# Conditioning weights of a two-layer decoder step: six vectors, loaded and placed otherwise

## The chip, the cores and the metric

One core of one Trainium2 chip. The metric is the device time of one execution in microseconds. The kernel before took 1056.21 us, the median of three runs (1053.03 to 1056.43).

## The reference

One step of a two-layer trunk for 256 prompt tokens and 8 sample tokens (264 columns, D = 1024). What the change touches is the conditioning at the head of each layer: six vectors of 1024 values for each of nine conditions (one prompt, eight samples), from a weight matrix of 1024 x 6144 (25.2 MB a layer).

```
def _layer(x, c, q_pos, lp, slopes, past):
    mod = einsum('bd,de->be', silu(c), lp['ada_w']) + lp['ada_b']
    sh1, sc1, g1, sh2, sc2, g2 = split(mod, 6)
    h = _rmsnorm(x, lp['norm1_g']) * (1 + sc1) + sh1
    proj = h @ lp['w_in']             # q, compressed/selected/window K and V, gates, z, x/B/C, dt
    kcmp, vcmp = _compress(k/v cache pages + new rows)     # blocks of 32, stride 16, small MLP
    o_att = gated sum of compressed, selected (top 16 blocks) and window attention
    y     = Mamba-2 scan over x/B/C, gated RMSNorm
    x = x + g1 * (concat[o_att, y] @ lp['w_out'])
    h2 = _rmsnorm(x, lp['norm2_g']) * (1 + sc2) + sh2
    ug, uv = split(h2 @ lp['ffn_w_up'])
    x = x + g2 * ((silu(causal_dwconv(ug)) * uv) @ lp['ffn_w_down'])
```

So vectors 0 and 1 (sh1, sc1) are needed before the projections, 2 (g1) at the output projection, 3 and 4 (sh2, sc2) at the second norm, and 5 (g2) at the down projection.

## The kernel before, in words

Activations lie feature by token: x is 128 partitions x 8 chunks x 264 tokens. Each weight tile (128x1024) is split on the chip into a high part (ACT copy, `whi`) and a low part (VectorE subtraction, `wlo`), and a product is three matmuls per chunk (`gemm8`): 24 matmuls of 264 columns to a projection tile.

The conditioning is `ada(l, r)`, a generator: three pieces r of 2048 columns. For each of 8 chunks k of the contraction four loads of 256 KB come in (`ada`, 128x512), and four matmuls with the 128x32 stationary silu(c) (`cs`) go to the four quarters of the array's columns, all into one PSUM bank, `psfl`. The four are a row here; a step of the generator (one `yield`) is a row. After the eighth row an ACT copy (`adam`), four transposes and one VectorE addition (`mod`) hand the piece over.

The stages stand in this order: compression of the cached pages of layer one (`compress`: units of two samples, 48 matmuls into `pso` each, pages in `cpg` tiles), with its first unit at the very start; the norm; projections (`w_in`, 6 + 10 tiles into `psmm`); attention and Mamba as several generators, stepped in the order of a written string SEQ; output projection; feed-forward (22 up pairs of tiles), in which layer two's compression units and its conditioning are stepped; down projection. The tile framework's scheduler then orders each engine's instructions by priority and dependence within these constraints, so the four matmuls of one row may come apart. Conditioning steps are called at: the start (piece 0 of layer one), the projections of layer one (piece 1, as `side`), its attention (piece 2, letter A of SEQ, as `fill`), its feed-forward (piece 0 of layer two, every other f), the down projection (DOWN = 5 rows of piece 1 of layer two), the head of layer two's projections (GAP = 3 rows and the rest as `side`), its attention (piece 2).

ADA_BUFS gives the buffers of the `ada` tag by pool: 6 in the compression pool, 4 in that of attention, 6 in the feed-forward's. Selected-cache pages (`page`) are fetched by `fetch` into a ring of 8. In the Mamba part the eight samples' B and C vectors are spread over partitions by a product with the identity (`bd`) and a ones matmul, one `bd` for each of eight pieces. Every engine instruction is issued by the helper `emit` and the trace gives its line, L117, to nearly all rows; the tile names tell them apart. Names: psfl conditioning, pso compression, psmm projections and other wide products, psat attention and small products.

Of the kernel before, what the change touches and what calls it, by code (L numbers as in the profile page):

```python
# [17 lines left out]
NL = 2  # L18
D = 1024
TP = 256  # L20
NS = 8
# [13 lines left out]
ADA_BUFS = {"cmp": 6, "att": 4, "ffn": 6}  # L35
# [67 lines left out]
def decode_step(ctx, tc, I, O):  # L103
# [199 lines left out]
    def ada(l, r):  # L303

        if r == 0:
# [4 lines left out]
        acc = fl()  # L310
        for k in range(KC):
            for g in range(4):
                name = pools_names[-1]
                t = sb([512], "ada", ADA_BUFS[name[:3]], F32, pools[-2] if name == "attn1" else pools[-1])
                load(t, I["ada"][l, r * KC + k, :, g, :])
                PE.matmul(acc[32 * g:32 * g + 32, :], cs[:, k, :], t, start=k == 0, stop=k == KC - 1)
                if g == 1 and HALF:
                    yield
            yield
        m = sb([512], "adam", 1)  # L320
        S.activation(m, acc, AF.Copy)
        tr = fl()
        for j in range(4):
            PE.transpose(tr[:, j * 128:(j + 1) * 128], m[:, j * 128:(j + 1) * 128], ident)
        V.tensor_tensor(MOD[l][:, r * 16:(r + 1) * 16, :].rearrange("p (g j) m -> p g j m", g=4),
                        tr.rearrange("p (j g m) -> p g j m", j=4, g=4)[:, :, :, 0:9],
                        MOD[l, "b"][:, r * 16:(r + 1) * 16].rearrange("p (g j) -> p g j", g=4)
                        .unsqueeze(3).to_broadcast([128, 4, 4, 9]), op=OP.add)
# [47 lines left out]
    def compress(l, both, bufs):  # L376
# [15 lines left out]
        def pages(s, kv):  # L392
            t = ph([NPG, 2 if both else 1, 128], "cpg", bufs)
            load_pages(t, I["cmpc"][l], s, 0 if both else kv, 2 if both else 1)
# [45 lines left out]
        for kv, sp in order:  # L440
            if kv not in W:
                weights(kv)
            if not both:
                raws = [pages(s, kv)[:, :, 0, :] for s in (2 * sp, 2 * sp + 1)]
            elif kv == 0:
                pair = [pages(s, 0) for s in (2 * sp, 2 * sp + 1)]
# [15 lines left out]
    def layer(l, A, pa, early, done, side, fill):  # L462
# [10 lines left out]
        for _ in range(GAP[l]):  # L473
            next(side, None)

# [110 lines left out]
        done()  # L586
        pb = begin(f"attn{l}")


        def slot(tag, shape, dt=F32):  # L590
            return sb(shape, tag, dict(whi=WB[0], wlo=WB[1], st=WB[2])[tag], dt)

        order = (0, 2, 4, 6, 1, 3, 5, 7)
        ring = []

        def fetch():
            n = len(ring)
            i, s = n // NS, order[n % NS]  # L600
            if i > 2:
                return
            t = ph([1024], "page", PAGES)
            if i == 2:
                load(t, I["wst"][l, s])
                store(O["wst"][l, s], t)
                v = t.rearrange("p (a c f) -> p a c f", a=2, c=4)
                ring.append((v[:, 0], v[:, 1]))
            else:
                v = t.rearrange("p (c a f) -> p c a f", a=2, c=4)  # L610
                load_pages(v, I["slcc"][l], s, 0, 2, 4 * i, 4)
                ring.append((v[:, :, 0, :], v[:, :, 1, :]))

        def samples():
# [24 lines left out]
            for _ in range(PAGES):  # L639
# [416 lines left out]
        def space_samples():  # L1056
# [26 lines left out]
            ys = small([4, NS], 1, "ys")  # L1083
            for g in range(2):
# [5 lines left out]
                for b in range(2):  # L1090
                    o = mb()
                    bd = small([NS, 64], 1, "bd")
                    V.tensor_tensor(bd[:8], bc[:8, b, 64 * g:64 * g + 64].unsqueeze(1).to_broadcast([8, NS, 64]),
                                    ident[:8, :8].unsqueeze(2).to_broadcast([8, NS, 64]), op=OP.mult)
                    PE.matmul(o, ones[:8, :], bd[:8].rearrange("p s n -> p (s n)"), start=True, stop=True)
# [88 lines left out]
        bg = [compress(l + 1, 0, 4), ada(l + 1, 0)] if l + 1 < NL else []  # L1184
        for f in range(NFF):
            if f % 2 == 0:
                for b in bg:
                    for _ in range(1 + UNITS * (f == 0 and b is bg[0])):
                        next(b, None)
# [22 lines left out]
        rest = ada(l + 1, 1) if l + 1 < NL else iter(())  # L1212
# [27 lines left out]
    units, third = compress(0, 1, 4), ada(0, 0)  # L1240
    for i in range(FIRST):
        next(units)
        if i == 0:
            load(cst, I["consts"])
            load(x, I["xT"])
        for _ in range(-(-8 // FIRST)):
            next(third, None)
    run(third)
    for k in range(KC):
        square(k)  # L1250
# [29 lines left out]
GAP = (0, 3)  # L1280
DOWN = 5
UNITS = 0
PINS = ()
HALF = 0
# [128 lines left out]
```

## Time and profile before

| | |
|---|---|
| median of 3 runs | 1056.21 us (1053.03 to 1056.43) |
| the profiled execution | 1060.55 us |
| its span | 1058.8 us |
| mean granted TensorE clock | 0.949 |
| busy: TensorE, VectorE, ACT, POOL | 979.6, 655.8, 486.3, 170.0 us |

The span is what the trace covers. The chain is the sequence of work that ended last, followed back from the last instruction; a stage is read from it by taking the chain of that stretch only. A matmul of the conditioning is two records, so a row of four shows as x8. In the chain "DMA ada" is time in which TensorE waited for a conditioning load and for nothing else.

### The profile page before, as it was taken

The numbers are of one execution on the slowest core, as the hardware profiler recorded it, in microseconds if no ns is written. First come the engines' busy times: TensorE is split into PE (matmuls) and PEld (weight loads), VectorE is DVE, ScalarE is ACT, GpSimd is POOL, SyncE is SP. The second block draws the span as 40 slices with busy tenths as digits, with TensorE's granted clock in tenths as the row PEclk, the third lists the DMA queues.
The fourth block names the chain that finished last, engine by engine and source line by source line (L and its number), as shares of the span: only waits on it lengthen the run. The fifth ranks groups of instructions, "written<-read, shape, count | busy, mean of one in ns | idle before, by whom it ended". The sixth has DMA issues, their size and how long they took to land.

```text
span 1058.8 us, 20737 instructions
## 1 busy us (share of the span) xinstructions
PE 979.6 (93%) x7480; PEld 795.0 (75%) x7480; DVE 655.8 (62%) x1427; ACT 486.3 (46%) x1036; POOL 170.0 (16%) x337
## 2 busy tenths in 40 slices
PE   3799999997997999999999989999799789999996
PEld 3238898652466899899998949965246689999995
DVE  2347554557657865766764558365865777777553
ACT  3225544332254554655553426453235456666441
POOL 0201001114213000101111103031421311111110
PEclk9899999897899899999999999999789889999998
DMA  8779668436847777765577568753694635555651
GB/s 279 262 240 304 227 211 280 162 128 203 333 158 222 225 219 232 255 195 193 185 233 236 165 223 262 250 180 126 207 339 152 208 100 180 181 180 182 195 171 41
DMA packets 115081, 220.33 MB, mean 208 GB/s; under 512 B 13218, under 2 KB 56098, under 8 KB 114850
## 3 DMA queue, kind: packets, MB, share of 16 engines
q1 hardware_dynamic: 110882, 205.29, 60.5%
q0 software_dynamic: 3520, 13.17, 3.1%
q8 instruction: 59, 0.97, 0.4%
q10 hardware_dynamic: 576, 0.54, 0.2%
q14 instruction: 44, 0.36, 0.1%
HBM read 204.70 MB, written 14.25 MB: 207 GB/s over the span
## 4 chain that ended last, share of the span: by engine, by line
PE 82%; DMA 6%; DVE 6%; ACT 2%; issue 2%; SPq 2%; POOL 0%; DVEq 0%; ACTq 0%; POOLq 0%
PE psmm L117 42%; PE psat L117 23%; PE pso L117 10%; PE psfl L117 8%; DMA ada<-in_ada_dram 3%; SPq L117 1%; DMA st<-in_cw_dram 1%; DVE wlo L117 1%; DMA st<-in_wup_dram 1%; DVE bd L117 1%; DMA cpg<-in_cmpc_dram 1%; DVE rs L117 1%; ACT whi L117 1%; DVE psm L117 0%; DVE st L117 0%
## 5 line engine op out<-in xcount | busy, mean ns | idle before, releaser
L117 DVE TENSOR_TENSOR wlo<-st,whi 128x1024 fp32r<-128x1024 f32 (+1 forms) x204 | 232.7, 1141 | 148.8 <-ACT whi L117 132.9
L117 ACT ACTIVATE whi<-st 128x1024 fp32r<-128x1024 f32 (+1 forms) x204 | 201.8, 991 | 231.0 <-PE psmm L117 163.3
L117 PE MATMUL psmm<-hhi,whi 128*128 128x264 f32 x800 | 233.3, 292 | 4.2 <-ACT hhi L117 2.6
L117 PE MATMUL psmm<-hhi,wlo 128*128 128x264 f32 x800 | 228.4, 286 | 0.8 <-DVE wlo L117 0.8
L117 PE MATMUL psmm<-hlo,whi 128*128 128x264 f32 x800 | 228.6, 286 | 0.0
L117 PEld LDWEIGHTS psmm<-hhi,whi 128*128 128x128 f32 x800 | 151.5, 190 | 22.3 <-issue 7.4
L117 PEld LDWEIGHTS psmm<-hhi,wlo 128*128 128x128 f32 x800 | 151.2, 189 | 3.0 <-DVE wlo L117 1.6
L117 PEld LDWEIGHTS psmm<-hlo,whi 128*128 128x128 f32 x800 | 151.9, 190 | 0.9 <-issue 0.7
L117 PE MATMUL psmm<-act,whi 128*128 128x264 f32 x704 | 128.7, 284 | 0.0
L117 PEld LDWEIGHTS psmm<-act,whi 128*128 128x128 f32 x704 | 108.8, 188 | 4.2 <-issue 3.4
L117 PE MATMUL psfl<-ada,cs 128*32 128x512 f32 x384 | 99.3, 648 | 11.0 <-DMA ada<-in_ada_dram 10.9
L117 PE MATMUL psat<-hhi,whi 128*128 128x264 f32 x352 | 100.8, 286 | 1.4 <-ACT whi L117 1.4
L117 PE MATMUL psat<-hhi,wlo 128*128 128x264 f32 x352 | 100.6, 286 | 1.0 <-DVE wlo L117 1.0
L117 PE MATMUL psat<-hlo,whi 128*128 128x264 f32 x352 | 100.5, 286 | 0.0
L117 PE MATMUL psmm<-act,wlo 128*128 128x264 f32 x352 | 99.9, 284 | 0.0
L117 PE MATMUL pso<-whi,cwh 128*128 128x252 f32 x256 | 76.3, 298 | 21.0 <-ACT whi L117 16.2
L117 PE MATMUL pso<-wlo,cwh 128*128 128x252 f32 x256 | 75.5, 295 | 0.1
L117 PE MATMUL pso<-whi,cwl 128*128 128x252 f32 x256 | 75.3, 294 | 0.0
L117 PEld LDWEIGHTS pso<-whi,cwh 128*128 128x128 f32 x256 | 51.3, 200 | 31.6 <-ACT whi L117 16.2
L117 PEld LDWEIGHTS psat<-hhi,whi 128*128 128x128 f32 x352 | 67.1, 191 | 1.6 <-ACT whi L117 1.6
L117 PEld LDWEIGHTS psat<-hhi,wlo 128*128 128x128 f32 x352 | 66.8, 190 | 1.2 <-DVE wlo L117 1.2
L117 PEld LDWEIGHTS psat<-hlo,whi 128*128 128x128 f32 x352 | 67.2, 191 | 0.0
(303 smaller groups left out, 1553.2 us busy)
## 6 DMA issues: line engine op xcount, KB each, us to landing
ada<-in_ada_dram SPq DMA_DIRECT2D x192, 256.0 KB, 4.4
st<-in_wup_dram SPq DMA_DIRECT2D x88, 512.0 KB, 3.6
st<-in_wdn_dram SPq DMA_DIRECT2D x44, 512.0 KB, 3.5
st<-in_win_dram SPq DMA_DIRECT2D x40, 512.0 KB, 4.6
page<-in_slcc_dram SPq DMA_DIRECT2D x128, 128.0 KB, 2.6
st<-in_cw_dram SPq DMA_DIRECT2D x16, 512.0 KB, 5.4
cpg<-in_cmpc_dram SPq DMA_DIRECT2D x64, 128.0 KB, 3.3
st<-in_wout_dram SPq DMA_DIRECT2D x32, 256.0 KB, 3.0
```

The lines of the kernel that those rows point to most:

```text
L117: ins = f(*a, **k)
```

## The change

Conditioning is computed in six vectors j of 1024 columns. A load is 128 x 4 x 256 floats (512 KB): one chunk k with all four quarters. Two chunks make a pair, which the new helper `together` issues as eight adjacent matmuls, those of the tile loaded later first. With `wide`, a pair lives in one of the page tiles (`cpg`, 4 buffers), else in two `ada` buffers; ADA_BUFS is now 3, 2 and 4. A step of the generator is a pair, four to a vector; each vector has a hand-off with two transposes.

The places: vectors 0 and 1 of layer one at the start, ahead of all pages and weights, x loaded first of all; 2 and 3 in its projections; 4 in its attention; 5 in its feed-forward, followed there by 0 and 1 of layer two; 2 of layer two in the down projection (DOWN = 4); 3 and 4 in layer two's projections; 5 in layer two's feed-forward; none in its attention. In layer two the attention pool is begun before the projections, and the selected pages are fetched in the loop of the q and kv tiles. The `bd` products are four of 8x1024, ahead of the loop of their users.

```diff
-ADA_BUFS = {"cmp": 6, "att": 4, "ffn": 6}
+ADA_BUFS = {"cmp": 3, "att": 2, "ffn": 4}
...
+    def together(calls):
+        for n, (out, w, a, start, stop) in enumerate(calls):
+            if n == 0:
+                PE.matmul(out, w, a, start=start, stop=stop)
+                continue
+            with tc.high_priority():
+                tc.keep_in_program_order(PE.matmul(out, w, a, start=start, stop=stop))
...
-    def ada(l, r):
+    def ada(l, js, wide=0):
...
-        acc = fl()
-        for k in range(KC):
-            for g in range(4):
...
-                load(t, I["ada"][l, r * KC + k, :, g, :])
-                PE.matmul(acc[32 * g:32 * g + 32, :], cs[:, k, :], t, start=k == 0, stop=k == KC - 1)
...
+        for j in js:
+            acc = fl()[:, :256]
+            for kk in range(0, KC, 2):
+                two = []
+                if wide:
+                    t = ph([2, 4, 256], "cpg", wide)
+                    two = [(kk, t[:, 0]), (kk + 1, t[:, 1])]
+                for k in (kk, kk + 1):
+                    name = pools_names[-1]
+                    if not wide:
+                        t = sb([4, 256], "ada", ADA_BUFS[name[:3]], F32, pools[-2] if name == "attn1" else pools[-1])
+                        two.append((k, t))
+                    load(two[k - kk][1], I["ada"][l, j, k])
+                together([(acc[32 * g:32 * g + 32, :], cs[:, k, :], t[:, g, :], k == 1, k == KC - 2)
+                          for k, t in reversed(two) for g in range(4)])
+                yield
...
+        pb = begin(f"attn{l}") if early is None else None
...
+            if pb is not None and len(ring) < PAGES:
+                fetch()
             o = mtile(I["win"][l, m], h)
...
+            bds = [ph([1024], "mam", 2) for _ in range(2)]
+            for g in range(2):
+                V.tensor_tensor(bds[g][:8].rearrange("p (b s n) -> p b s n", b=2, s=NS),
...
-                    bd = small([NS, 64], 1, "bd")
...
-                    PE.matmul(o, ones[:8, :], bd[:8].rearrange("p s n -> p (s n)"), start=True, stop=True)
+                    PE.matmul(o, ones[:8, :], bds[g][:8, 512 * b:512 * b + 512], start=True, stop=True)
...
-        bg = [compress(l + 1, 0, 4), ada(l + 1, 0)] if l + 1 < NL else []
+        bg = [compress(l + 1, 0, 4), chain(ada(l, (5,)), ada(l + 1, (0, 1)))] if l + 1 < NL else [iter(()), ada(l, (5,))]
         for f in range(NFF):
             if f % 2 == 0:
...
+                next(bg[0], None)
+            if f % 2 == 0 or f < 4:
+                next(bg[1], None)
...
-        rest = ada(l + 1, 1) if l + 1 < NL else iter(())
+        rest = ada(l + 1, (2, 3)) if l + 1 < NL else iter(())
...
-    units, third = compress(0, 1, 4), ada(0, 0)
-    for i in range(FIRST):
+    units = compress(0, 1, 4)
+    load(x, I["xT"])
+    shift = ada(0, (0, 1), 4)
+    for k in range(KC - 1):
+        square(k)
+    for _ in range(3):
+        next(shift)
+    load(cst, I["consts"])
+    square(KC - 1)
+    run(shift)
+    for _ in range(FIRST):
         next(units)
...
-    rest = layer(0, A, pa, lambda: units, lambda: end(p0), ada(0, 1), [ada(0, 2)])
+    rest = layer(0, A, pa, lambda: units, lambda: end(p0), ada(0, (2, 3)), [ada(0, (4,))])
     pa = begin("att1")
-    layer(1, pools[-1], pa, None, lambda: None, rest, [ada(1, 2)])
+    layer(1, pools[-1], pa, None, lambda: None, chain(rest, ada(1, (4,))), [])
...
-GAP = (0, 3)
-DOWN = 5
+GAP = (0, 0)
+DOWN = 4
```

What stands on SP, the queue that issues the loads, at the start before: after three small ones the weights of the first compression unit (`cw`), then its pages, one DMA each.

```order
L117 DMA st_93<-in_cw_dram 128x1024
L117 DMA st_97<-in_cw_dram 128x1024
L290 TENSOR_LOAD pt
L117 ISA
L117 DMA cpg_101<-in_cmpc_dram 128x256
```

The same place in the changed kernel, where `cst` is the constants:

```order
L117 DMA x_66<-in_xT_dram 128x2112
L117 DMA adab_112<-in_adab_dram 128x48
L117 DMA cpg_115<-in_ada_dram 128x1024 x2
L117 DMA cpg_126<-in_ada_dram 128x1024 x2
L117 DMA cpg_137<-in_ada_dram 128x1024 x2
L117 DMA cst_61<-in_consts_dram 128x1581
L117 DMA cpg_154<-in_ada_dram 128x1024 x2
L117 DMA cpg_172<-in_ada_dram 128x1024 x2
L117 DMA cpg_183<-in_ada_dram 128x1024 x2
L117 DMA cpg_194<-in_ada_dram 128x1024 x2
L117 DMA cpg_205<-in_ada_dram 128x1024 x2
L117 DMA st_226<-in_cw_dram 128x1024
```

Sixteen conditioning loads in eight pairs of 1 MB stand where weights and pages stood. On TensorE, before, in the second compression unit, single conditioning matmuls stand between those of the unit:

```order
L117 MATMUL psfl_227<-ada_246,cs_70 32x512
L117 MATMUL pso_513<-wlo_515,cwh_112_503 128x252
L117 MATMUL pso_513<-whi_514,cwl_113_504 128x252
L117 MATMUL psfl_227<-ada_249,cs_70 32x512
L117 MATMUL pso_513<-whi_514,cwh_112_503 128x252
L117 MATMUL pso_513<-wlo_515,cwh_112_503 128x252
L117 MATMUL psfl_227<-ada_252,cs_70 32x512
L117 MATMUL psfl_227<-ada_255,cs_70 32x512
```

TensorE's first rows in the changed kernel:

```order
L117 MATMUL psfl_114<-cpg_115,cs_70 32x256 x8
L117 MATMUL psfl_114<-cpg_126,cs_70 32x256 x8
L117 MATMUL psfl_114<-cpg_137,cs_70 32x256 x8
L117 MATMUL psat_151<-row_74,cst_61 1x264
L117 MATMUL psat_151<-s_24_149,cst_61 1x264
L117 MATMUL psat_367<-cst_61,row_74 128x1 x3
L117 MATMUL psfl_114<-cpg_154,cs_70 32x256 x8
```

All pairs of the first two vectors, eight matmuls each, stand ahead of the first compression unit, with the sums of the norm (`psat`) between them. On SP in the changed kernel, in layer two's projections, weight tiles (`win`), conditioning pairs and pages alternate:

```order
L117 DMA st_7933<-in_win_dram 128x1024
L117 DMA cstin_7674<-in_convst_dram 128x192
L117 DMA ada_7685<-in_ada_dram 128x1024
L117 DMA ada_7687<-in_ada_dram 128x1024
L117 DMA st_7990<-in_win_dram 128x1024
L299 TENSOR_LOAD pt
L117 ISA
L117 DMA page_8050<-in_slcc_dram 128x256
L117 ISA
L117 DMA page_8050<-in_slcc_dram 128x256
L117 DMA ada_7742<-in_ada_dram 128x1024
L117 DMA ada_7744<-in_ada_dram 128x1024
```

A pair takes both `ada` buffers of that pool. Before, the same queue had pages between the weight tiles of this stage as well:

```order
L117 DMA st_8030<-in_win_dram 128x1024
L290 TENSOR_LOAD pt
L117 ISA
L117 DMA page_8460<-in_slcc_dram 128x256
L117 ISA
L117 DMA page_8460<-in_slcc_dram 128x256
L117 ISA
L117 DMA page_8460<-in_slcc_dram 128x256
L117 DMA st_8062<-in_win_dram 128x1024
```

Pages stand between weight tiles in both; the conditioning pairs are new there. TensorE at the head of layer two's attention, before, with a row of conditioning among the small products:

```order
L117 MATMUL psat_8395<-dta_7709,cst_61 128x16
L117 MATMUL psat_8400<-xc_7714 128x128 x2
L117 MATMUL psfl_8403<-ada_8404,cs_70 32x512
L117 MATMUL psfl_8403<-ada_8407,cs_70 32x512
L117 MATMUL psfl_8403<-ada_8410,cs_70 32x512
L117 MATMUL psfl_8403<-ada_8413,cs_70 32x512
L117 MATMUL psat_8420<-gates_7681,cst_61 128x24
L117 MATMUL psat_8426<-kc_3864,qz_72 32x63 x8
```

The same place in the changed kernel:

```order
L117 MATMUL psat_8575<-dta_7672,cst_61 128x16
L117 MATMUL psat_8580<-xc_7677 128x128 x2
L117 MATMUL psat_8587<-gates_7644,cst_61 128x24
L117 MATMUL psmm_8522<-hhi_7550,whi_8516 128x264
L117 MATMUL psmm_8522<-hlo_7551,whi_8516 128x264
L117 MATMUL psmm_8522<-hhi_7550,wlo_8517 128x264
L117 MATMUL psat_8593<-kc_3812,qz_72 32x63 x8
```

The row of conditioning is gone from there, and matmuls of the z projection stand in its place.

## Rows read from the trace of the kernel before

**Rows 1.** Page, parts 1 and 4: busy time; shares of the chain by line.

```profile
PE 979.6 (93%) x7480; PEld 795.0 (75%) x7480; DVE 655.8 (62%) x1427; ACT 486.3 (46%) x1036; POOL 170.0 (16%) x337
...
PE psmm L117 42%; PE psat L117 23%; PE pso L117 10%; PE psfl L117 8%; DMA ada<-in_ada_dram 3%; SPq L117 1%; DMA st<-in_cw_dram 1%; DVE wlo L117 1%; DMA st<-in_wup_dram 1%; DVE bd L117 1%; DMA cpg<-in_cmpc_dram 1%; DVE rs L117 1%; ACT whi L117 1%; DVE psm L117 0%; DVE st L117 0%
```

**Rows 2.** Chain of 0 to 100 us: start, us on the chain, engine, tile.

```profile
32.95 3.22 DMA ada<-in_ada_dram
...
44.71 0.97 PE psfl L117 x2
...
82.57 5.60 PE pso L117 x48
...
91.89 1.00 PE psfl L117 x8
```

**Rows 3.** Windows: us; busy of PE, PEld, DVE, ACT, POOL; clock; DMA share; GB/s.

```profile
0.00:30.00 30.00, 11.63 (x60) 8.76 (x60) 8.94 (x18) 8.57 (x14) 1.99 (x10) 1.00 0.87 279
30.00:60.00 30.00, 25.65 (x84) 9.24 (x84) 8.50 (x20) 7.32 (x15) 5.37 (x7) 0.83 0.75 251
240.00:270.00 30.00, 24.12 (x110) 9.37 (x103) 23.58 (x44) 7.98 (x24) 11.99 (x10) 0.73 0.72 223
270.00:300.00 30.00, 29.16 (x192) 13.42 (x191) 18.26 (x62) 12.79 (x43) 8.07 (x16) 0.98 0.89 343
870.00:900.00 30.00, 30.00 (x250) 30.00 (x250) 23.91 (x44) 19.10 (x37) 4.54 (x16) 1.00 0.57 179
```

**Rows 4.** Chain of 175 to 345 us, layer one's attention: shares, then steps.

```profile
by line: PE psat L117 30.6%; PE psmm L117 26.6%; PE psfl L117 9.4%; PE pso L117 6.0%; DMA ada<-in_ada_dram 5.8%; SPq L117 3.0%; issue 2.8%; DVE bd L117 2.3%; DVE psm L117 1.5%; DVE st L117 1.5%; DVE wlo L117 1.2%; ACT psc L117 1.1%; ACT whi
...
179.82 6.31 DMA ada<-in_ada_dram
186.18 1.91 PE psfl L117 x2
...
189.10 2.11 PE psfl L117 x6
...
218.53 3.61 DMA ada<-in_ada_dram
```

**Rows 5.** Chain of 686 to 862 us, layer two's attention: shares by line.

```profile
by line: PE psat L117 31.5%; PE psmm L117 28.1%; PE psfl L117 7.7%; PE pso L117 5.9%; DMA ada<-in_ada_dram 4.1%; issue 3.8%; DVE bd L117 2.2%; DVE x L117 2.0%; DVE wlo L117 1.6%; DVE psm L117 1.5%; DVE st L117 1.5%; DVE rs L117 1.2%; ACT ps
```

**Rows 6.** Timeline of PE, 731.7 to 732.4 us: start, us, instruction, shapes.

```profile
731.77 0.86 PE L117 MATMUL psat<-st,s 128*32 128x128 f32 x24
```

**Rows 7.** DMA issues: count, KB of one, median us from issue to landing.

```profile
ada<-in_ada_dram SPq DMA_DIRECT2D x192, 256.0 KB, 4.4
...
st<-in_cw_dram SPq DMA_DIRECT2D x16, 512.0 KB, 5.4
cpg<-in_cmpc_dram SPq DMA_DIRECT2D x64, 128.0 KB, 3.3
...
x<-in_xT_dram SPq DMA_DIRECT2D x1, 1056.0 KB, 9.2
```

**Rows 8.** Page, part 5: the splits of weight tiles on ACT.

```profile
L117 ACT ACTIVATE whi<-st 128x1024 fp32r<-128x1024 f32 (+1 forms) x204 | 201.8, 991 | 231.0 <-PE psmm L117 163.3
```

**Rows 9.** Timeline of DVE in the norm of layer two.

```profile
623.11 0.22 DVE L117 TENSOR_TENSOR ts<-ts,psmm 128x64 f32<-128x64 f32 x1 [2.75 <-PE psmm L117]
...
629.30 0.89 DVE L117 SCALAR_TENSOR_TENSOR hlo<-s,mod,hhi 128x256 fp32r<-128x256 f32 x2 [0.18 <-ACT hhi L117]
```

**Rows 10.** Timeline of the SP queue, 0 to 24 us.

```profile
3.96 9.04 SPq L117 DMA_DIRECT2D cpg<-in_cmpc_dram  x16
```

**Rows 11.** Chain of 175 to 345 us again: the first of the bd products.

```profile
246.64 2.10 DVE bd L117
```

**Rows 12.** Chain of 345 to 430 us, head of layer one's feed-forward.

```profile
405.53 8.09 DMA st<-in_wup_dram
```

**Rows 13.** Chain of 600 to 700 us, down projection to layer two's projections.

```profile
614.29 4.62 DMA ada<-in_ada_dram
...
638.12 44.96 PE psmm L117 x372
```

More of the change, by code (lines that the diff above doesn't have):

```diff
@@ L301, in run @@
             pass
-    def ada(l, r):
-        if r == 0:
+    def ada(l, js, wide=0):
+        if l not in MOD:
             MOD[l] = sb([48, 9], "mod", 2)
@@ L320, in ada @@
[L320 to L328, printed above, removed]
+        for j in js:
[14 more added lines that the diff above has]
+                yield
+            m = sb([256], "adam", 1)
+            S.activation(m, acc, AF.Copy)
+            tr = fl()
+            for i in range(2):
+                PE.transpose(tr[:, i * 128:(i + 1) * 128], m[:, i * 128:(i + 1) * 128], ident)
+            V.tensor_tensor(MOD[l][:, 8 * j:8 * j + 8, :].rearrange("p (g i) m -> p g i m", g=4),
+                            tr[:, :256].rearrange("p (i g m) -> p g i m", i=2, g=4)[:, :, :, 0:9],
+                            MOD[l, "b"][:, 8 * j:8 * j + 8].rearrange("p (g i) -> p g i", g=4)
+                            .unsqueeze(3).to_broadcast([128, 4, 2, 9]), op=OP.add)
@@ L390, in weights, with pages @@
             W[kv] = (whi, wlo)
-        def pages(s, kv):
+        def pages(s, kv, n):
             t = ph([NPG, 2 if both else 1, 128], "cpg", bufs)
-            load_pages(t, I["cmpc"][l], s, 0 if both else kv, 2 if both else 1)
+            load_pages(t[:, :, :n], I["cmpc"][l], s, kv, n)
             return t
@@ L443, in compress @@
             if not both:
-                raws = [pages(s, kv)[:, :, 0, :] for s in (2 * sp, 2 * sp + 1)]
+                raws = [pages(s, kv, 1)[:, :, 0, :] for s in (2 * sp, 2 * sp + 1)]
             elif kv == 0:
-                pair = [pages(s, 0) for s in (2 * sp, 2 * sp + 1)]
+                pair = [pages(s, 0, 2) for s in (2 * sp, 2 * sp + 1)]
             if both:
@@ L474, in layer, with slot, fetch @@
             next(side, None)
+        pb = begin(f"attn{l}") if early is None else None
+        def slot(tag, shape, dt=F32):
+            return sb(shape, tag, dict(whi=WB[0], wlo=WB[1], st=WB[2])[tag], dt)
+        order = (0, 2, 4, 6, 1, 3, 5, 7)
+        ring = []
+        def fetch():
+            n = len(ring)
+            i, s = n // NS, order[n % NS]
+            if i > 2:
+                return
+            t = ph([1024], "page", PAGES)
+            if i == 2:
+                load(t, I["wst"][l, s])
+                store(O["wst"][l, s], t)
+                v = t.rearrange("p (a c f) -> p a c f", a=2, c=4)
+                ring.append((v[:, 0], v[:, 1]))
+            else:
+                v = t.rearrange("p (c a f) -> p c a f", a=2, c=4)
+                load_pages(v, I["slcc"][l], s, 0, 2, 4 * i, 4)
+                ring.append((v[:, :, 0, :], v[:, :, 1, :]))
         first = iter(()) if early is None else early()
@@ L585, in layer @@
         run(side)
[L586 to L612, printed above, removed]
+        if pb is None:
+            done()
+            pb = begin(f"attn{l}")
         def samples():
@@ L638, in samples @@
             V.tensor_copy(slf, selfp[:, :2])
-            for _ in range(PAGES):
+            while len(ring) < PAGES:
                 fetch()
@@ L1279 @@
 CYCLE = "PMZSPAMPSMPBMZ"
-GAP = (0, 3)
-DOWN = 5
-UNITS = 0
+GAP = (0, 0)
+DOWN = 4
 PINS = ()
-HALF = 0
 FIRST, EARLY = 1, 1
@@ L1301, in _layout @@
     A["cT"] = ca(c.reshape(32, KC, 128).transpose(2, 1, 0))
-    A["ada"] = ca(f["ada_w"].reshape(NL, KC, 128, 3, 2048).transpose(0, 3, 1, 2, 4)).reshape(NL, 24, 128, 4, 512)
+    A["ada"] = ca(f["ada_w"].reshape(NL, KC, 128, 6, 4, 256).transpose(0, 3, 1, 2, 4, 5))
     A["adab"] = ca(f["ada_b"].reshape(NL, 48, 128).transpose(0, 2, 1))
```

20 lines of the change are left out of this document (2 added, 18 removed).

## The prediction

> **What bounds the kernel now.** I read the busy shares and the chain first: TensorE is busy 93% of the span, and of the chain that ended last 42% are its matmuls into psmm, 23% psat, 10% pso, 8% psfl [rows 1]. psfl is the conditioning: 128x32 stationary silu(c) against 512 columns, four matmuls per row of work, one in each quarter of the columns of the array. The chain by time shows two prices for it. All four together (x8 records) hold the chain 1.00 us; one alone (x2) holds it 0.97 [rows 2]. So a lone quarter costs as much as four, and from 36 to 67 us TensorE works off the quarters of the first piece alone or in twos between compression matmuls, though the last of their loads that is on the chain is there at 36.2; the stretch 30 to 60 has 0.75 of DMA share and the clock at 0.83 [rows 2, 3]. The same tile is on the chain inside both attention stages, mostly as a wait for its load: psfl 9.4% and its DMA 5.8% of 170 us in layer one, 7.7% and 4.1% of 176 us in layer two [rows 4, 5], so 25.8 and 20.8 us. The feed-forward stages are TensorE at full clock with no gap (870 to 900: 30.00 of 30.00) [rows 3]. There every row of work that is added is paid.
>
> **The change part by part.** I sum against the profiled execution, 1060.55 us (its span is 1058.8); the median shown is 1056.21, so 4.3 come off at the end. A pair below is two rows of 4x256 columns, the same columns as one row of 4x512 now. That half the columns take half the time is seen on other narrow matmuls: 24 records of 128 columns, four abreast, take 0.86 us [rows 6], 0.14 for each of six passes, where 512 columns need 0.49 (0.97 over two). So a pair costs 1.0 where both loads are there, and there are 48 pairs as there were 48 rows; what changes is that none is torn apart, and where they stand.
>
> *Start.* x and vectors 0 and 1 now come before all pages. In order on SP: x, the two vectors (of 12 that the 192 loads of 256 KB make now, 4,096 KB each), the constants, 1 MB of compression weights, 16 pages, two more conditioning loads and the second 1 MB of weights: 1,056 + 8,192 + 790.5 (128x1581 floats) + 1,024 + 2,048 + 1,024 + 1,024 KB, with some 660 KB of small loads 15,820 KB or 16.2 MB [rows 7]. The first 30 us moved 279 GB/s at a share of 0.87 [rows 3]: 320 at a full share. 16.2 MB take 51 us and 3 for the start, so the weights of the second unit are there at 54. The norm's vector operations stand behind their split on VectorE: two ACT copies of 0.99 and a last subtraction of about the same [rows 8], 3, then 8 us for the norm with a GELU in it (623.1 to 630.2 in layer two [rows 9], plus 1): 65. Left before the third unit are 32 compression matmuls (3.8), one tile of 24 (2.9), a pair (1.0) and a gap: 73.5. Before, this unit starts at 82.57 [rows 2] with the same work done, so -9. Bounds: at 251 GB/s, the stretch 30 to 60 as it is, it would be 87 (+5); at 343, the most that any 30 us move (270 to 300), about 70 (-13) [rows 3]. I take the full-share rate because the new head is 19 large loads, where 16 page loads now hold the queue for 9.04 us [rows 10].
>
> *Projections of layer one.* Vectors 2 and 3 stand where the second piece stood: 8 pairs for its 8 rows. One more hand-off (ACT copy, transposes, VectorE add, new accumulator in the one psfl bank), about 1 us where little hides it: +1 (0 to +3).
>
> *Attention of layer one.* Four pairs for eight rows, in the places of the first four. These keep their price: the wait at 179.82 (6.31 us), the two pieces behind it (1.91 and 2.11) and three whole rows of 1.0, 13.3. The rest of the 25.8 goes, 12.5, from the wait at 218.53 (3.61) on [rows 4]. VectorE is at 23.6 of 30 there [rows 3] and takes over part of the chain; I take -9, bounds -12.5 and 0. The eight small products bd become four of twice the size, ahead of the loop: the first takes 2.10 on the chain [rows 11]; it gets longer, the later three leave the chain. 0 (-2 to +1.5 in each layer).
>
> *Feed-forward of layer one.* Vector 5 is added: four pairs, 4.0, two more hand-offs, 2, and 2 MB more of loads per 20 us of the first units where the chain already waits for loads (405.53, 8.09 us) [rows 12], say 2: +8 (+2 to +14). Down projection: four pairs for five rows, one of which was held by its load: -2.
>
> *Projections of layer two.* The norm goes 1 us sooner and the first tile is no longer torn by lone quarters: before, psfl and its loads (614.29, 4.62) fill the time to 638.12, and half of the first tile's 24 matmuls come after that, so it ends at 639.6 [rows 13]. Without them the norm would end at 629 and the tile at 633.5: -6. But eight pairs stand in this stage now, six between tiles that run at 2.9 (44.96 us for 372 matmuls [rows 13]): +6, hand-offs +2. And each pair has only two buffers: its two loads are issued only when the pair before is done, and SP is in order, so projection tiles and pages stand behind a waiting conditioning load. Two tiles and a pair take 6.8 us on TensorE and need 1 MB + 1 MB + 0.5 MB of pages, 8.2 us at 320 GB/s. Half of that shortfall over six pairs: +4. Sum +6, bounds -3 (all of it hidden) and +16 (every pair waits some 2 us more). That pages are fetched here brings nothing by itself: in the order of before SP has them between the same tiles already.
>
> *Attention of layer two.* No conditioning is left: up to 20.8 [rows 5]. With VectorE, ACT and the samples' chain right behind, -15, bounds -3 and -20.8. *Feed-forward of layer two:* four pairs and a hand-off in a stage with no gap: +5 (+3 to +8).
>
> Sum: -9 +1 -9 +8 -2 +6 -15 +5 = -15. 1060.55 - 15 = 1045.5, and 1041 on the level of the median.
>
> **The rivals.** *Low clock at the start* (10%). While vectors 0 and 1 arrive TensorE works in bursts of one pair or two per megabyte. Between 240 and 270 us, where it waits for VectorE, the granted clock is 0.73, a mix of 2.4 and 1.2 GHz [rows 3]. At 1.2 the first unit's 48 matmuls (5.60 [rows 2]) take twice that: +6, 1047. The Trainium skill, "TensorE: Matmul & The Clock Gate", section "HAM oscillation — how this bites in real kernels", says the same of kernels whose bursts are shorter than the load they wait for, that each burst starts cold; against it, the first 30 us here show 1.00 with 11.6 us of work in them [rows 3].
>
> *All of it realized* (18%): attention gives back 12.5 and 20.8, the loads hide, the start gains 13, the layer-two projections cost 2: -13 +1 -12.5 +5 -2 +2 -20.8 +5 = -35, 1021. For it: TensorE is the chain in most of the pieces of both stages. Against: the products bd and the softmax on VectorE are in them too [rows 3, 11].
>
> *The chains behind take over* (10%): only a third of the 24 us in attention is won: +16, 1057, no change. For it: VectorE 23.6 of 30.
>
> *The pair of buffers becomes the bound* (12%). Place: layer two's projections. If a pair's loads, issued after the pair before, land more than the 5.8 us of two tiles later, TensorE stands, and so do the tiles queued behind. From 9 us on, six times 3 us eat the gain; at 10 it is 24 in place of 4, 1061, slower. For it: such loads took 4.62 and 6.31 us on the chain with half as much beside them [rows 4, 13]. Against: at the rate of the first 30 us a megabyte takes less than 4 us [rows 3].
>
> *Four abreast is not what happens at 256 columns* (3%): a row of four costs 1.0 whatever its width. 80 rows after the start in place of 40 are +40, 1081. The 128-column row [rows 6] speaks against it.
>
> **How the numbers follow.** The forecast itself gets 47%: 1041, its own range 1030 to 1052. About 0.3%, 3 us, is what a measurement of this kernel can tell from no change. Faster: the forecast, the low clock and the full gain, and a little of the third rival, less the edge of the forecast: 0.77. Same: most of "chains behind": 0.09. Slower: the buffers, four abreast, and what I have not seen: 0.14. The range 1020 to 1059 leaves out the last two rivals and the tail beyond the full gain.
>
> **What would show it.** In the profile after: psfl in runs of 16 records of 1.0 us, none of two; psmm of the first projection at 67 to 71 us and the third unit near 73; psfl near 8% of the chain of attention one and none in attention two, each stage shorter by 9 and 15; the layer-two projections ending not much earlier after the norm than before, with DMA waits on ada in them. The forecast is wrong if the third unit starts after 82, if psfl's waits in layer two's projections exceed 15 us, or if attention two is less than 5 us shorter with the waits moved to VectorE.

## The result

The changed kernel took 1042.71 us, the median of 14 runs (1033.74 to 1050.77), against 1056.47 of the kernel before (14 runs, 1053.03 to 1065.11): ratio 0.9852, with a 95% interval of 0.9817 to 0.9886. The ratio goes by the fast runs alone, those within 1.5% of the fastest of the same kernel (12 of the changed kernel's 14), so it is not the quotient of the two medians. The forecast was 1041, with a range of 1020 to 1059. Its profiled execution took 1040.78 us, span 1039.0. A second profile of the same kernel, taken later beside other runs (e8 below), took 1048.78 us, span 1047.0. By stages, in us, with the granted clock in brackets where it differs (the limits are read off the timelines: end of the first projection tile, end of the sixteenth, first operation of the next norm on the samples, first down matmul):

| stage | before | changed | changed again | forecast of the change |
|---|---|---|---|---|
| start, to the first tile | 82.6 | 71.2 | 70.1 | -9 |
| projections of layer one | 90.7 | 91.4 | 91.3 | +1 |
| attention one | 167.3 (0.89) | 153.6 (0.95) | 167.0 (0.83) | -9 |
| feed-forward one | 204.1 | 209.0 | 209.9 | +8 |
| down projection one | 70.7 | 68.9 | 68.9 | -2 |
| projections of layer two | 67.8 | 74.4 | 75.5 | +6 |
| attention two | 158.7 (0.93) | 150.7 (0.88) | 146.1 (0.91) | -15 |
| feed-forward two | 139.1 | 141.8 | 140.6 | +5 |
| down projection two, end | 77.9 | 77.9 | 77.9 | 0 |
| sum of the stages | 1058.8 | 1038.9 | 1047.1 | -15 |

The page of the changed kernel, busy time and the chain by line:

```profile
PE 949.7 (91%) x7864; PEld 803.7 (77%) x7864; DVE 650.7 (63%) x1429; ACT 487.4 (47%) x1042; POOL 167.8 (16%) x337
...
PE psmm L117 40%; PE psat L117 22%; PE pso L117 10%; PE psfl L117 4%; DMA st<-in_cw_dram 3%; DMA ada<-in_ada_dram 3%; DVE wlo L117 2%; DMA cpg<-in_ada_dram 2%; DMA st<-in_wup_dram 1%; DMA page<-in_wst_dram 1%; DVE s L117 1%; SPq L117 1%; ACT whi L117 1%; DVE rs L117 1%; ACT psc L117 1%
```

TensorE's busy time fell by 29.9 us (by 19.1 in the second profile, at a lower clock) and psfl's share of the chain from 8% to 4% [rows 1], while loads of conditioning and of compression weights came onto it.

The chain of the changed kernel's start (start, us, what), which answers to [rows 2]:

```profile
12.68 9.71 DMA cpg<-in_ada_dram
22.40 11.64 DMA st<-in_cw_dram
...
42.65 7.84 DMA st<-in_cw_dram
50.51 1.07 ACT cwh L117
...
64.04 3.81 PE pso L117 x32
...
71.33 1.00 PE psfl L117 x16
```

The weights of the second unit are there at 50.5 us (forecast 54); a pair, 16 records, costs 1.00 us. The stretches that answer to [rows 3] (columns as there):

```profile
0.00:30.00 30.00, 14.66 (x130) 6.12 (x130) 3.66 (x19) 4.90 (x12) 5.81 (x15) 0.94 0.94 363
30.00:60.00 30.00, 17.12 (x113) 11.63 (x114) 17.23 (x38) 14.00 (x25) 0.37 (x2) 0.72 0.86 280
```

The head moves 363 and then 280 GB/s, 321 over the first 60 us, where the sum took 320; until the weights are there, at 50.5 us, the mean is 334. The third unit starts at 72.1 (70.9 in the second profile; forecast 73.5, before 82.4). The clock of 30 to 60 us is 0.72, as the rival on the low clock had it, but the chain there is a wait for weights: in the second profile the clock of that stretch is 0.83, and the third unit still starts some 21.7 us after the weights, as here. The Trainium skill, "TensorE: Matmul & The Clock Gate", section "HAM oscillation — how this bites in real kernels", says of a kernel whose bursts of matmuls are shorter than its wait for the next load that each burst starts cold, at the lower clock. This trace agrees: TensorE stands idle for 8.0 us before 42.6, and its next matmuls start 0.21 us apart, then 0.12 from 47.7 on. It shows no cost of this in time, since the weights end last.

The DMA issues (count, KB of one, median us to landing) against [rows 7]:

```profile
ada<-in_ada_dram SPq DMA_DIRECT2D x80, 512.0 KB, 5.2
...
cpg<-in_ada_dram SPq DMA_DIRECT2D x16, 512.0 KB, 9.4
```

Half as many loads of twice the size. The first sixteen take 9.4 us (median), in a stretch where the DMA share is 0.94.

The chain of layer two's projections, against [rows 13]:

```profile
by line: PE psmm L117 44.5%; DMA ada<-in_ada_dram 28.2%; PE psfl L117 12.8%; PE psat L117 4.3%; DVE rs L117 2.7%; DVE wlo L117 2.7%; issue 2.1%; ACT whi L117 1.4%; DVE row L117 0.6%; ACT s L117 0.5%; DVE ts L117 0.3%; DVE mod L117 0.0%
...
616.93 5.39 DMA ada<-in_ada_dram
622.36 1.11 PE psfl L117 x16
...
629.57 7.15 DMA ada<-in_ada_dram
```

And the SP queue of the same place (start, us, loads):

```profile
616.50 0.81 SPq L117 DMA_DIRECT2D ada<-in_ada_dram  x2
617.51 0.88 SPq L117 DMA_DIRECT2D page<-in_slcc_dram  x2
618.48 0.38 SPq L117 DMA_DIRECT2D st<-in_win_dram  x1
623.06 0.81 SPq L117 DMA_DIRECT2D ada<-in_ada_dram  x2
```

Each pair of loads is issued while the pair before is being worked off (from 615.8 and 622.4 on), and everything behind it waits with it: the pair of buffers does hold the queue, as the step said. The stage is 6.6 and 7.7 us longer (forecast +6). What TensorE itself was idle for in this stage (total us, times, longest) has a line for these loads that is far smaller than their 28.2% of the chain:

```profile
PE psfl L117 <- DMA ada<-in_ada_dram: 2.6, 3, 1.4
```

While the chain stands on such a load, TensorE works on projection tiles (from 616.8 us on, for instance). So "DMA ada" on the chain is not, as was said ahead of the prediction, time in which TensorE waits for nothing else.

Attention two, against [rows 5]:

```profile
by line: PE psat L117 30.0%; PE psmm L117 28.2%; PE pso L117 8.1%; DMA page<-in_wst_dram 7.2%; DVE wlo L117 3.6%; ACT psc L117 3.6%; issue 3.4%; ACT whi L117 2.1%; ACT pT L117 1.7%; DVE x L117 1.6%; DVE mam L117 1.6%; DVE pp L117 1.1%; DVE 
...
752.46 10.99 DMA page<-in_wst_dram
```

psfl is gone from it. A wait for the window pages stands there, 11.0 us, which the chain of before does not have. It is in the chain of this stage in the second profile, e2 and e4 too, with 6.1 us in e1, and not in e3, e7 and e9.

### The profile page after: what moved, and what is told of

It reads as the page before. It is cut to its first block, busy times and chain, and to the rows that moved or that the text cites. A ratio compares the mean times of both kernels' runs of the same rounds, so it can differ in the third digit from the quotient of the medians.

```text
span 1039.0 us, 21345 instructions
## 1 busy us (share of the span) xinstructions
PE 949.7 (91%) x7864; PEld 803.7 (77%) x7864; DVE 650.7 (63%) x1429; ACT 487.4 (47%) x1042; POOL 167.8 (16%) x337
## 4 chain that ended last, share of the span: by engine, by line
PE 76%; DMA 11%; DVE 7%; ACT 3%; issue 2%; SPq 1%; POOL 0%; DVEq 0%; ACTq 0%; POOLq 0%
PE psmm L117 40%; PE psat L117 22%; PE pso L117 10%; PE psfl L117 4%; DMA st<-in_cw_dram 3%; DMA ada<-in_ada_dram 3%; DVE wlo L117 2%; DMA cpg<-in_ada_dram 2%; DMA st<-in_wup_dram 1%; DMA page<-in_wst_dram 1%; DVE s L117 1%; SPq L117 1%; ACT whi L117 1%; DVE rs L117 1%; ACT psc L117 1%
## 5 line engine op out<-in xcount | busy, mean ns | idle before, releaser
L117 POOL COPY fout<-xr 128x26 f32<-128x26 f32 x44 | 28.1, 639 | 247.0 <-ACT xr L117 247.0
L117 PEld LDWEIGHTS psmm<-act,wlo 128*128 128x128 f32 x352 | 66.1, 188 | 0.0
```

The costliest lines, as they stand in the source:

```text
L117: ins = f(*a, **k)
```

## The experiments

Each is a kernel of its own, timed against the kernel before on the same chip.

**e1, the rows held together and nothing else** (the kernel before):

```diff
-                PE.matmul(acc[32 * g:32 * g + 32, :], cs[:, k, :], t, start=k == 0, stop=k == KC - 1)
+                four.append((acc[32 * g:32 * g + 32, :], cs[:, k, :], t, k == 0, k == KC - 1))
+            together(four[::-1])
```

> The kernel before with one edit: the four matmuls of a conditioning row stand together, behind its last load; loads, pieces and places as before. Theory A (the quarters torn apart at the start are what the change saved there; where the loads stand matters little): the 26 quarters that cost about 0.97 us each between 36 and 67 us become six or seven rows of 1.0, so the third compression unit starts 10 to 18 us sooner than at 82.4, and the whole is near 1042. Theory B (the early loads are what counts): the third unit starts at 78 or later, the whole at 1050 or above. Both: attention of layer two 3 us shorter at most, since its rows and their load waits stay.

Measured: 1073.54 us, ratio 1.0159 (1.0105 to 1.0213), slower. Neither theory. The third unit did start at 70.3, but out of its place: the norm came some 7 us later, and the first projection tile ended at 89.9, not 82.6. Of the 13.4 us between the spans 7.3 lie there and 6.7 in the attention stages. The chain of e1's start shows why:

```profile
32.32 3.51 DMA ada<-in_ada_dram
35.87 2.06 PE psfl L117 x8
...
38.25 4.02 DMA ada<-in_ada_dram
42.31 2.06 PE psfl L117 x8
```

A whole row waits for four loads, and the last of these are issued only when the row before has given back its buffers: 6.4 us a row from 35.87 to 42.31. The row itself takes 2.06 where it took 1.00 [rows 2], at a granted clock of 0.66 to 0.69 in 40 to 70 us, so the clock is part of the loss. In the kernel before the queue of the same place reads

```profile
32.95 34.91 SPq L117 DMA_DIRECT2D ada<-in_ada_dram  x32
```

32 loads in 34.9 us. There the queue waits for TensorE, not TensorE for the queue. Two windows of the kernel before (columns as in [rows 3]), and what SP waited for from 15 to 72 us (total us, times, longest):

```profile
40.00:50.00 10.00, 10.00 (x33) 2.97 (x34) 0.17 (x1) 0.00 (x0) 0.25 (x1) 0.87 0.58 181
50.00:60.00 10.00, 10.00 (x41) 3.83 (x41) 2.90 (x14) 0.63 (x1) 0.00 (x0) 1.00 0.75 254
...
SPq L117 <- PE psfl L117: 17.1, 16, 2.2
```

TensorE has no gap, and from 36.2 to 67.5 us it waits for no conditioning load. So the lone quarters did hold TensorE. But each also gave its buffer back by itself, and with six buffers that kept the loads going. Held together without more or earlier loads, the rows make TensorE wait instead: 13.1 us for conditioning loads from 32 to 75 us.

**e2, the start of before in the changed kernel:**

```diff
-    load(x, I["xT"])
-    shift = ada(0, (0, 1), 4)
...
+    for _ in range(FIRST):
+        next(units)
+    load(cst, I["consts"])
+    load(x, I["xT"])
+    run(ada(0, (0, 1)))
...
```

> The changed kernel with the first compression unit, its weights and pages ahead of vectors 0 and 1 again, and these in ada buffers (three, one load each) and not in the page tiles. Theory A (pairs that stay whole are the gain): third unit at 72 to 76 us as in the changed kernel, the time within 4 us of 1042.7. Theory B (the early loads): it starts at 80 or later, the time 1050 or more. The rest of the kernel should keep its lengths within 3 us in both.

Measured: 1054.85 us, 0.9935 (0.9894 to 0.9976). The first projection tile ends at 82.4, as before the change, though all pairs are whole; the projections then end 8.3 us later than in the changed kernel (170.8 against 162.6). Theory B: whole pairs alone gain nothing at the start. The edit takes away both the place in front of the queue and the four tiles of a megabyte, so which of the two the start owes its gain to is not shown; no run has the old order with more buffers.

**e3, vector 4 of layer two back in its attention:**

```diff
-    layer(1, pools[-1], pa, None, lambda: None, chain(rest, ada(1, (4,))), [])
+    layer(1, pools[-1], pa, None, lambda: None, rest, [ada(1, (4,))])
```

> The changed kernel with vector 4 of layer two computed in its attention (four pairs at the first A places), not in its projections. If a pair costs its 1.0 us and its wait in both stages: projections of layer two 6 us shorter (74.4 to 68), attention two 4 to 8 longer (150.7 to 156), the time the same within 3. Theory 'hidden' (attention two was shortened less than forecast, because its conditioning stood in waits for pages and VectorE anyway): projections 6 shorter, attention 0 to 2 longer, the time 1038. Theory 'clock' (the granted clock fell to 0.50 from 718 to 748 us because TensorE has less to do there): the same 1038, and the clock of the stage back above 0.92.

Measured: 1044.26 us, 0.9843 (0.9768 to 0.9919). Projections of layer two 66.4 (8 to 9 us shorter), attention two 150.5 at a clock of 0.92. e7 below, with none there, took 144.9 at 0.92, so four pairs cost 5 to 6 us in attention at like clock, and 8 to 9 in the projections, where the pair of buffers waits: so about a tie, as the first theory said. The whole does not tell it apart from the changed kernel.

**e4, the pages fetched late again** (`pb = None` in place of the early pool):

> The changed kernel with layer two's attention pool begun behind its projections and the pages fetched there, as before. The prediction's step says that fetching them in the projections brings nothing: time 1042.7 within 3 us, attention two within 2 of 150.7. The rival, that the early pages are worth something: attention two 3 to 6 us longer; or that they get in the way of the conditioning loads: projections of layer two 3 to 5 shorter, since 4 MB fewer stand between the pairs.

Measured: 1044.31 us, 0.9866 (0.9819 to 0.9914); attention two 149.4 at a clock of 0.90, projections 73.0. The early pages bring nothing in sum, as the step said. Without them between the pairs the projections are 1.5 and 2.6 us shorter; attention two is about 2 us longer than a line through the changed kernel's two profiles gives at 0.90 (147.6).

**e5, thirteen matmuls without use in each attention stage:**

```diff
-        for c in SEQ[l]:
+        for i, c in enumerate(SEQ[l]):
             next(bg[c], None)
+            if 50 <= i <= 62:
+                PE.matmul(fl(), ident, cst[:, :512], start=True, stop=True)
```

> The changed kernel with 13 added matmuls in each attention stage (128x128 stationary, 512 columns, constants in, nothing reads them), one after each of the steps 50 to 62 of the order string, which puts them some 50 to 85 us into the stage. There four profiles of kernels with one and the same attention one showed the granted clock at 0.50 for 8 to 40 us, and the stage took 154 us (mean clock 0.95) to 166 (0.84). Theory 'clock' (with less conditioning in it the stage has less for TensorE to do, the clock falls and takes back part of the gain): the clock of that stretch stays above 0.85, attention one at 150 to 156 and attention two at 143 to 148, the time 1030 to 1040. Rival (the clock there does not hang on such work, or the added matmuls are on the path): both stages longer by 6 to 13 us each, the time 1055 to 1065.

Measured: 1056.79 us, 0.9972 (0.9938 to 1.0006), 8 us slower than the changed kernel beside it (e8). The two attention stages in e5 (span, us, then busy times as in [rows 3]):

```profile
162.87:332.05 169.18, 154.17 (x1153) 96.86 (x1152) 104.20 (x288) 66.12 (x190) 42.27 (x66) 0.92 0.51 173
...
688.43:837.21 148.78, 140.60 (x1090) 90.13 (x1088) 103.37 (x284) 62.93 (x180) 42.74 (x66) 0.95 0.49 171
```

The stages did not shorten: the rival on the time. On the clock only attention two speaks for the theory, 0.95 where the changed kernel has 0.88 and 0.91. Attention one's 0.92 lies within what the changed kernel shows without added work (0.95, and 0.83 in e8); it is 12 us longer than that kernel at like clock (the line of e8 gives 157.0 at 0.92), about what the 13 added matmuls come to (26 records there, of 0.59 us each, partly overlapping).

**e6, vectors 4 and 5 of both layers in attention** (and two A moved in the order string):

```diff
-        bg = [compress(l + 1, 0, 4), chain(ada(l, (5,)), ada(l + 1, (0, 1)))] if l + 1 < NL else [iter(()), ada(l, (5,))]
+        bg = [compress(l + 1, 0, 4), ada(l + 1, (0, 1))] if l + 1 < NL else [iter(()), iter(())]
...
-    rest = layer(0, A, pa, lambda: units, lambda: end(p0), ada(0, (2, 3)), [ada(0, (4,))])
+    rest = layer(0, A, pa, lambda: units, lambda: end(p0), ada(0, (2, 3)), [ada(0, (4, 5))])
...
-    layer(1, pools[-1], pa, None, lambda: None, chain(rest, ada(1, (4,))), [])
+    layer(1, pools[-1], pa, None, lambda: None, rest, [ada(1, (4, 5))])
```

> The changed kernel with vectors 4 and 5 of both layers in the attention stages: eight pairs there, at places 5, 15, 27, 39, 44, 50, 54, 59 of the order string, none in layer two's projections beyond vector 3, none of vector 5 in the feed-forward stages. Theory (a pair costs 1.0 to 2.0 us where TensorE is full, and 0.5 or less in attention's waits): projections of layer two 8 us shorter than 74.4, the two feed-forward stages 4 and 4 shorter than 209 and 142, attention one 161 and attention two 149 longer by 4 and 6: the time 1035 to 1040. Rival (in attention a pair costs its 1 us and the wait for its load): attention longer by 8 and 16, the time 1046 to 1055.

Measured: 1047.54 us, 0.9889 (0.9837 to 0.9940), within noise of e8. Projections 65.4, but attention two 162.1 at 0.88 where the changed kernel had 150.7 at that clock: eight pairs cost 11 us there. Attention one took 166.8 at 0.88, where the line of e8 gives 161.4: four pairs more cost 5 us. The feed-forward stages gave back only 1.2 to 2.2 and 0.2 to 1.5 us. Attention lies between the theory (4 and 6) and the rival (8 and 16), and the time is the rival's.

**e7, eight bd products in the loop again:**

```diff
...
-                    PE.matmul(o, ones[:8, :], bds[g][:8, 512 * b:512 * b + 512], start=True, stop=True)
+                    bd = small([NS, 64], 1, "bd")
+                    V.tensor_tensor(bd[:8], ..., op=OP.mult)
+                    PE.matmul(o, ones[:8, :], bd[:8].rearrange("p s n -> p (s n)"), start=True, stop=True)
```

> The changed kernel with the eight products bd of 8x512 in the loop, as before, in place of four of 8x1024 ahead of it. The prediction's step (worth -2 to +1.5 us a layer, taken as 0): time within 3 us of 1042.7, each attention stage within 3 us of the changed kernel's at the same granted clock. Rival (the four larger ones took VectorE off the path): each attention stage 4 to 6 us longer, the time 1050.

Measured: 1048.58 us, 0.9935 (0.9893 to 0.9978), against 1048.71 of the changed kernel beside it (e8). Attention one is 159.5 at 0.91 (the line of e8: 158.1), attention two 144.9 at 0.92. Worth nothing, as taken.

**e8, the changed kernel once more:**

> The changed kernel once more, for a second profile of it and for times on the same chip as the other three. If the spread of its times (1033.7 to 1050.8) comes from the granted clock in the attention stages, its stages other than these repeat within 1 us and attention one lies on the line of 1.1 us for each 0.01 of clock through 153.7 at 0.95 and 166.1 at 0.84; if it comes from elsewhere, other stages differ by 3 us or more.

Measured: 1048.71 us, 0.9899 (0.9848 to 0.9950). Attention one in the first profile of the changed kernel

```profile
162.57:316.22 153.65, 134.54 (x1127) 89.80 (x1126) 105.64 (x288) 66.20 (x190) 42.61 (x66) 0.95 0.57 191
```

and in e8

```profile
161.37:328.32 166.95, 151.94 (x1125) 96.23 (x1124) 106.01 (x289) 66.41 (x191) 43.45 (x66) 0.83 0.52 175
```

Same instructions, 13.3 us apart, 0.12 of clock: 1.1 us for each 0.01, the line expected. e3 (162.3 at 0.87) and e4 (166.1 at 0.84), with the same order of matmuls in this stage, lie on it. All other stages except attention two repeat within 1.3 us, a little over the 1 us expected. So most of the spread between the two profiles goes with the granted clock of the attention stages. The 14 runs of the result agree: the mean clock is 0.952 in the fastest (1033.74) and 0.931 in the slowest (1050.77).

**e9, the third piece of both layers not computed** (the kernel before; a constant stands for vectors 4 and 5):

```diff
+            V.memset(MOD[l][:, 32:48, :], 0.5)
...
-    rest = layer(0, A, pa, lambda: units, lambda: end(p0), ada(0, 1), [ada(0, 2)])
+    rest = layer(0, A, pa, lambda: units, lambda: end(p0), ada(0, 1), [])
...
-    layer(1, pools[-1], pa, None, lambda: None, rest, [ada(1, 2)])
+    layer(1, pools[-1], pa, None, lambda: None, rest, [])
```

> The kernel before with the third piece of both layers (vectors 4 and 5) not computed: a constant of 0.5 stands in its place, so the eight rows, their 64 loads of 256 KB and the hand-off are gone from both attention stages and nothing else is moved. It measures by itself what the prediction took as 25.8 and 20.8 us on the chain. Theory 'as forecast' (most of a row's share of the chain comes back): attention one 150 (from 167.3), attention two 140 (from 158.7). Theory 'clock takes back' (with them the clock of the middle of the stage falls to 0.50 and the wait for pages and VectorE follows): attention one 158 to 163 at a mean clock of 0.86 or less, attention two 147 to 152.

Measured: 1038.56 us, 0.9814 (0.9783 to 0.9845). Attention one and two in e9:

```profile
172.98:325.36 152.38, 132.53 (x1060) 89.90 (x1059) 103.52 (x288) 65.40 (x189) 41.48 (x66) 0.90 0.50 167
...
667.47:818.98 151.51, 130.70 (x1059) 88.81 (x1057) 103.87 (x287) 65.23 (x187) 42.78 (x66) 0.89 0.47 158
```

Attention one 14.9 us shorter at a clock of 0.90 (before 0.89); attention two 7.2 shorter at 0.89 (before 0.93). e1, with the same rows (held together) in attention two, took 163.3 there at 0.90, so at like clock the piece cost about 12. The chain's 25.8 and 20.8 were upper ends: (14.9 + 12) / (25.8 + 20.8), 58%, came back. One reason is that the chain counts the loads in full: 5.8% of 170 us and 4.1% of 176 us, 9.9 and 7.2 us [rows 4, 5], where TensorE itself was idle for them 4.4 and 2.5 us. Neither theory alone: in attention one the clock took nothing back.

**e10, vectors 2 and 3 in the down projection, 4 in attention:**

```diff
-DOWN = 4
+DOWN = 9
```

(and e3's edit)

> The changed kernel with vectors 2 and 3 of layer two both in the down projection of layer one (DOWN = 9) and vector 4 in its attention: no pair is left in layer two's projections. A pair costs 1.2 us in the down projection (its loads have four buffers there) and about 2.0 in the projections, where it waits for its loads. Theory: down projection 4.8 to 6 us longer than 68.9, projections of layer two 58 to 61 (from 74 to 75; 66.4 with vector 4 alone gone), attention two 150: the time 3 to 6 us below the changed kernel's, 1037 to 1042. Rival: the down projection's weights and the conditioning share the queue and the stage grows by 10: no gain.

Measured: 1046.37 us, 0.9834 (0.9794 to 0.9874). Down projection 73.9 (+5.0), projections 63.2 (-11 to -12), attention two 156.7 at 0.88. The first two came as the theory had them, within 3 us; attention two is 6 us longer than the 150 expected, at a lower clock than e3's, and the time of 1037 to 1042 did not come.

**e11, the same with late pages** (e10's edits and e4's):

> The same as e10, and the pages of layer two's attention fetched behind the projections, as before. With no pairs in the projections the pages have the queue to themselves there in e10, so if early pages are worth anything without conditioning between them, this is 2 to 5 us slower than e10; if they bring nothing, as the prediction's step says, the two agree within 3 us, about 1037 to 1042.

Measured: 1037.58 us (6 runs, 1033.12 to 1041.84), 0.9803 (0.9771 to 0.9836), the best of all. Down projection, projections of layer two and attention two in e11:

```profile
527.17:601.05 73.88, 73.62 (x650) 67.84 (x646) 34.01 (x53) 26.75 (x34) 7.70 (x8) 1.00 0.73 241
601.05:663.54 62.49, 56.83 (x454) 52.46 (x455) 41.49 (x93) 30.97 (x63) 9.76 (x23) 0.95 0.80 260
663.54:815.16 151.62, 139.63 (x1125) 89.62 (x1123) 103.35 (x286) 64.61 (x187) 41.02 (x66) 0.90 0.53 180
```

Those two stages together take 136.4 us, where the changed kernel's two profiles have 143.3 and 144.4; attention two is some 3 us longer than the changed kernel's at like clock. About 4 us, then, of the ratio's advance over 0.9852 and 0.9899. Its interval overlaps that of the first, not that of the second, and the kernels were not run on the same chip. The medians of e10 and e11 are 8.8 us apart, which neither expectation had, and in favour of late pages; early pages bring nothing here either. Most of the difference goes with the clock: of the 14.1 us between the spans of e10 and e11 (1047.7 and 1033.6), 10.1 lie in the attention stages, at a lower clock in e10 (161.5 and 156.7, both at 0.88; e11 156.5 at 0.93 and 151.6 at 0.90).

## Why the prediction was right, and where its sizes were off

*Start.* Right in size (11.4 and 12.5 to the first tile, 10.3 and 11.6 to the third unit, forecast 9) and in the rate that sets it, 321 for 320 GB/s. The opening reading, that from 36 to 67 us TensorE works off lone quarters, holds: it had no gap there. What it left out is that the loads stand close behind. Whole rows lose 7 us at the start when nothing else changes (e1), and whole pairs in the old order gain nothing (e2). The sum was not touched, because it went by bytes. One argument against the low clock does not hold: the 1.00 of the first 30 us [rows 3] is the clock column's, but in that trace the compression matmuls start 0.21 us apart from 17 to 22 us and 0.12 behind that.

*Attention one.* Forecast -9 (0 to -12.5). The profile's -13.7 is 7 at like clock (the line of e8 gives 160.3 at 0.89) and the rest a lucky draw of the clock; e8 got back 0.3. e9 shows that all eight rows cost 14.9. So half of them is worth about 7.5, and the 9 was near, although it was cut down from 12.5 for another reason, VectorE.

*Attention two.* Forecast -15 (-3 to -20.8), measured 8.0 and 12.6. Here the clock is the larger part of the shortfall: it is 0.93 in the profile of before and 0.88 and 0.91 in these two. At one and the same clock, e1 (all rows, 163.3) and e4 (none, 149.4, pages late in both) differ by 13.9:

```profile
689.96:853.23 163.27, 143.37 (x1127) 92.00 (x1125) 106.58 (x289) 66.08 (x188) 42.92 (x66) 0.90 0.57 191
...
679.89:829.28 149.39, 135.46 (x1076) 91.61 (x1074) 100.89 (x284) 64.07 (x186) 40.66 (x66) 0.90 0.51 178
```

e9's piece alone gives about 12. So the term was 1 to 3 us too large, no more. The new wait for the window pages does not explain it: e7, without it in the chain, takes 144.9 at 0.92, and the line through the changed kernel's two profiles, which have it, gives 144.6 there. That the chains behind take over, the third rival, is not shown.

*What is added.* These terms were the ones mis-sized. Feed-forward one is +4.9 and +5.8 for +8, feed-forward two +2.7 and +1.5 for +5; e6, without vector 5 there, is only 0.2 to 2.2 us shorter in either. The hand-offs, priced at 1 us each, do not show there, and in feed-forward two not even four pairs at 1.0 us do. "A stage with no gap" was read from one window: over the whole stage TensorE was busy 134.5 of 139.1 us before. Why a pair costs less than 1 us there is not shown. Projections of layer two are +6.6 and +7.7 for +6. bd and early pages are 0, as taken (e7, e4).

One sign that the prediction gave for being wrong did come: waits for conditioning loads hold 21.4 us of the chain in layer two's projections (28.8% of 74.4), over its 15. It was a poor sign, because TensorE was idle for these loads for only 2.6 us. The rival of the pair of buffers has the right mechanism and not the price.

*The sum.* The two profiles give -19.9 and -11.7 for -15, and the medians -13.8. That the total came so near is in part luck. The start and the two feed-forward stages came out 8 to 9 us better together than forecast, and the clock of the attention stages moves the time by more than that from one execution to the next.

What stayed open: why the clock of the middle of an attention stage is at 0.50 for some 7 us at a stretch in one execution and for 40 in another with the same instructions. No run here settles it.

## What to carry to other kernels

Before packing instructions together, look at what gives back the buffers of their loads. Here an untidy order held the engine, but it also freed the buffers one by one; whole rows paid only together with larger and earlier loads. The share of the chain that a piece of work holds was an upper end of what its removal gave (58% came back here); leaving it out for one run gives the price. The chain's time on a load is not the engine's idle time: ask the view of waits for that. Where a stage's clock varies, compare stages at like clock before giving a gain, or a shortfall, to the change.

## What the hardware showed

Two executions of the same part of attention one, 55 to 80 us into the stage. In e8 (us, busy times, clock, as in [rows 3]):

```profile
217.00:225.00 8.00, 5.97 (x48) 4.14 (x50) 3.63 (x12) 1.86 (x4) 0.00 (x0) 0.50 0.70 206
225.00:233.00 8.00, 7.62 (x35) 4.53 (x33) 4.19 (x5) 1.60 (x6) 1.90 (x1) 0.50 0.70 203
233.00:241.00 8.00, 8.00 (x16) 1.17 (x14) 7.76 (x12) 1.43 (x7) 3.10 (x2) 0.50 0.46 138
```

In the first profile of the changed kernel:

```profile
218.00:226.00 8.00, 5.62 (x68) 4.11 (x67) 4.04 (x13) 2.16 (x6) 0.00 (x0) 1.00 0.66 184
226.00:234.00 8.00, 6.27 (x31) 2.46 (x30) 6.87 (x9) 1.30 (x5) 1.90 (x1) 0.66 0.73 207
234.00:242.00 8.00, 8.00 (x24) 2.04 (x20) 6.83 (x11) 1.86 (x8) 3.52 (x4) 0.91 0.80 252
```

In the last row of each, TensorE counts as busy for 8.00 of 8.00 us: with 16 matmuls at a clock of 0.50, and with 24 at 0.91. A full busy share does not tell how much work was done; read it together with the count and the clock.
